# Scale and shift of three norms moved from a GpSimd run to a VectorE job that advances between weight splits

## The chip, the cores and the metric

The kernel runs on one core of one Trainium2 chip. A core has five engines that each take their own list of instructions in order and wait for one another by semaphores: TensorE (PE, matrix products), VectorE (DVE), ScalarE (ACT), GpSimd (POOL) and SyncE (SP, which here only issues transfers). The metric is the device time of one execution in microseconds (us), as the median of several runs.

## The reference

One layer of a streaming encoder on 256 frames of width 2048, all in float32. `P` below is a block of 128 rows; the residual stream `x` is normalised four times.

```
x = LN(x) * ln_in_g + ln_in_b
mix = concat(mLSTM heads, conv channels, chunked attention heads)(x @ w_in) @ w_out
x = LN(ALPHA * x + mix) * ln1_g + ln1_b
ca = softmax((x @ xq) @ k^T) @ v @ xo            # k, v = mem @ xkv
x = LN(ALPHA * x + ca) * ln2_g + ln2_b
gate, val = x @ ffn_w_up ; gate = causal_conv3(gate)
x = LN(ALPHA * x + (gelu(gate) * val) @ ffn_w_down) * ln3_g + ln3_b
```

## The kernel before

**Precision.** Every large product is made of three products of float32r parts: a matrix is split into `hi` (a rounded copy) and `lo` (the rest), and hi·hi, hi·lo and lo·hi are added up. The activations are split once. The weights stream through: `load_w` fetches a tile `raw` (three buffers, filled by transfers that SP issues), and cuts it into two halves; for each half ACT casts `hi` and DVE subtracts `lo` (function `split`, line 156), into four pairs of buffers (seven in the feed-forward part). So a half is ready for TensorE when its `lo` is, and a `raw` buffer is free for the next transfer when both of its halves have been split.

**The two forms of product.** `tm_part` (line 209) takes the weights as the moving operand and needs `lo` at its second matmul of a half. `cm_chunk` (lines 176 and 182) takes them as the stationary operand, with the eight hi matmuls of a half first and the eight lo matmuls behind; in the feed-forward part it holds all lo matmuls of a chunk back behind its four hi halves.

**Jobs.** Work that belongs beside the products (norms, attention heads, the convolution) is written as generators in the list `jobs`. Each product calls `tick` once per half, and `tick` advances every job by one step. Within an engine a scheduler then sets the final order, with a few instructions pinned by `keep_in_program_order`, all of POOL's transfers among them (`pool_load`).

**The stage in question.** The residual stream lies in `xt` as two tiles of 128 tokens by 2048 columns. What the products read next is a transposed copy that gets its scale and shift in ACT (`ln_transpose`), so TensorE never waits for the scale and shift of `xt` itself: `xt` needs it only by the next residual sum, hundreds of microseconds later. `ln_affine` does this for the input norm, the norm behind the mixer and the norm behind the cross attention, once the normalised stream is transposed. For each of four blocks of 512 columns (called rounds below) POOL loads the scale row and the shift row, copied to all partitions, into the single buffer `gb` (the two transfers are called the scale load and the shift load below), then multiplies and adds for both token tiles: 16 instructions of 128x512 for a norm on POOL, which has little else to do there.

The first norm's run lies under the first part of the input projection. There `tm_part` takes the weights in eight halves of 784 columns, eight of 768 and four of 1024, called the first to the twentieth half below; the second run lies under the key projection (`cm_chunk`), the third under the first chunks of the feed-forward part.

Of the kernel before, what the change touches and what calls it, by code (L numbers as in the profile page):

```python
# [52 lines left out]
def trunk_kernel(ctx: ExitStack, tc: tile.TileContext, plan, x, memT, wts, pvec, rows, gbias, abias, normg, out):  # L53
    nc = tc.nc
    V, A, G = nc.vector, nc.scalar, nc.gpsimd
# [81 lines left out]


    jobs = []

    def tick():
        for j in list(jobs):
            if next(j, jobs) is jobs:
                jobs.remove(j)

    def drain():
        while jobs:
            tick()
# [15 lines left out]
    def cm_chunk(a, mat, c0, c1, dst, loaded=None):  # L164

        ps = mm.tile([P, 2, 2, S], F32, name="mm")
        cols = [slice(j * P, (j + 1) * P) for j in range(2)]  # L170
        held = 4 if len(homes) > 4 else 1
        lows = []
        for ks, wH, wL in loaded or cm_load(mat, c0, c1):
            for kk, k in enumerate(ks):
                for j, cs in enumerate(cols):
                    nc.tensor.matmul(ps[:, j], lhsT=wH[:, kk, cs], rhs=a[:, k], start=(k == 0), stop=(k == KT - 1),  # L176
                                     skip_group_check=True)
            lows += [(k, wL[:, kk]) for kk, k in enumerate(ks)]
            if len(lows) == held * len(ks):
                for k, w in lows:  # L180
                    for j, cs in enumerate(cols):
                        nc.tensor.matmul(ps[:, j, 0, :], lhsT=w[:, cs], rhs=a[:, k, 0, :], start=False,  # L182
                                         stop=(k == KT - 1), skip_group_check=True)
                lows = []
            tick()
        cm_close(ps, dst)
# [11 lines left out]
    def tm_part(ps, a, mat, ks, cols, first=True, last=True, row0=0):  # L198

        n = sum(b - a for a, b in cols)  # L200
        kg = 8 if n <= 256 else 4
        for g in range(0, len(ks), kg):
            for kl, wH, wL in load_w(mat, [row0 + k for k in ks[g:g + kg]], cols):
                for kk, kr in enumerate(kl):
                    k = kr - row0
                    for tt in range(NT):
                        tsl = slice(tt * P, (tt + 1) * P)
                        for i, (part, w) in enumerate(((0, wH), (0, wL), (1, wH))):
                            nc.tensor.matmul(ps[tt][:, :n], lhsT=a[:, k, part, tsl], rhs=w[:, kk, :],  # L209
                                             start=(first and k == ks[0] and i == 0), stop=(last and k == ks[-1] and i == 2))  # L210
                tick()
# [95 lines left out]
    def ln_job(a, names, ri, wait):  # L307
        mv, rs = ln_scales(4)
        ln_normalise(mv, rs, 0)
        for _ in range(wait):  # L310
            yield
        for c in range(4):
            if c < 3:
                ln_normalise(mv, rs, c + 1)
            for k2 in range(4 * c, 4 * c + 4, 2):
                ln_transpose(a, names[0], names[1], k2)
            yield
        ln_affine(ri, rs)

    def pool_load(dst, src):  # L320

        tc.keep_in_program_order(G.dma_start(dst, src))
# [3 lines left out]
    def ln_affine(ri, begin):  # L326

        begun.append(tc.keep_in_program_order(G.tensor_copy(small.tile([P, NT], F32, name="begun"), begin)))
        for c in range(4):
            gb = lnp.tile([P, 2, 512], F32, name="gb")  # L330
            for i in range(2):
                pool_load(gb[:, i, :], rows[ri + i, c * 512:(c + 1) * 512].partition_broadcast(P))
            for tt in range(NT):
                sl = xt[:, tt, c * 512:(c + 1) * 512]
                G.tensor_mul(sl, sl, gb[:, 0, :])  # L335
                G.tensor_add(sl, sl, gb[:, 1, :])  # L336


    def load_mem(mp, g):
# [359 lines left out]


    def residual(ps, c, cols, first=True, last=True, tts=range(NT)):
        n = cols[c][1] - cols[c][0]
        for tt in tts:
            sl = xt[:, tt, cols[c][0]:cols[c][1]]
            if first:
                V.scalar_tensor_tensor(sl, sl, ALPHA, ps[tt][:, 0:n], ALU.mult, ALU.add)
            else:
                V.tensor_add(sl, sl, ps[tt][:, 0:n])
            if last:
                V.bn_stats(stats[:, tt, c, :], sl)  # L710

    mp = act_parts()
    for c in range(2):
        tm_part(ps01[c], mix, "w_out", list(range(4)), [COLS[c]], first=False)
        load_mem(mp, c)
        residual(ps01[c], c, COLS)
    for c in range(2, 4):
        ps = tm_open()
        tm_part(ps, mix, "w_out", list(range(KT)), [COLS[c]])
        load_mem(mp, c)  # L720
        residual(ps, c, COLS)
# [75 lines left out]
    for c in range(2):  # L797
        tm_part(ps01[c], op, "xo", list(range(12, 16)), [COLS_LAST[c]], first=False)
        residual(ps01[c], c, COLS)
# [3 lines left out]
    with tc.tile_pool(name="pre", bufs=1) as pre:  # L803
# [43 lines left out]
        behind.extend([[split0[3][0], split1[1]]] * 2 + [split1] * 2)  # L847
        up1 = list(cm_load("up", P, DFF + P))
    ln_affine(4, xp[:, KT - 1, 1, S - NT:S].bitcast(F32))


# [36 lines left out]
    for tt in range(NT):  # L888
        for c in (3, 4):
            n = COLS_LAST[c][1] - COLS_LAST[c][0]  # L890
            sl = xt[:, tt, COLS_LAST[c][0]:COLS_LAST[c][1]]
# [3 lines left out]
        for c in range(4):  # L895
            cs = slice(c * 512, (c + 1) * 512)
            sl = xt[:, tt, cs]
# [53 lines left out]
```

## Time and profile before

| | |
|---|---|
| median of three runs | 1525.84 us (1525.41 to 1526.14) |
| the profiled execution, its own time | 1525.82 us |
| its span, first to last instruction | 1523.6 us |
| TensorE busy | 1506.2 us, 99% of the span |
| VectorE busy | 1022.2 us, 67% |
| ScalarE busy | 764.3 us, 50% |
| GpSimd busy | 134.9 us, 9% |
| mean granted TensorE clock | 0.997 of full speed |

A busy share says how much of the span an engine had an instruction in it. TensorE's matmuls overlap, and one that waits inside a run of others shows as a gap between two starts. What a stall of another engine costs is therefore read from the starts of TensorE's rows, against the time at which each operand was ready.

### The profile page before, as it was taken

The numbers are of one execution on the slowest core, as the hardware profiler recorded it, in microseconds if no ns is written. First come the engines' busy times: TensorE is split into PE (matmuls) and PEld (weight loads), VectorE is DVE, ScalarE is ACT, GpSimd is POOL, SyncE is SP. The second block draws the span as 40 slices with busy tenths as digits, with TensorE's granted clock in tenths as the row PEclk, the third lists the DMA queues.
The fourth block names the chain that finished last, engine by engine and source line by source line (L and its number), as shares of the span: only waits on it lengthen the run. The fifth ranks groups of instructions, "written<-read, shape, count | busy, mean of one in ns | idle before, by whom it ended". The sixth has DMA issues, their size and how long they took to land.

```text
span 1523.6 us, 20632 instructions
## 1 busy us (share of the span) xinstructions
PE 1506.2 (99%) x8254; PEld 1314.2 (86%) x8254; DVE 1022.2 (67%) x1346; ACT 764.3 (50%) x1000; POOL 134.9 (9%) x133
## 2 busy tenths in 40 slices
PE   9999999999999999999999999999999999999996
PEld 7998888888888888998898888888888888888886
DVE  7875999688686545665678765566656665566666
ACT  6554454685454445554455643455435554455541
POOL 0460001000006300000027000000000000000000
PEclk9999999999999999999999999999999999999998
DMA  8585555454656654435647555545554545545451
GB/s 342 177 263 198 184 188 181 153 197 163 238 199 216 217 197 169 163 139 193 221 162 226 222 182 205 193 166 209 185 192 186 195 179 196 206 166 211 169 190 66
DMA packets 46351, 293.39 MB, mean 193 GB/s; under 512 B 5484, under 2 KB 6128, under 8 KB 15536
## 3 DMA queue, kind: packets, MB, share of 16 engines
q1 hardware_dynamic: 42768, 282.12, 50.6%
q0 software_dynamic: 2768, 8.66, 2.8%
q8 instruction: 64, 1.05, 0.3%
q10 hardware_dynamic: 720, 1.31, 0.2%
q14 instruction: 31, 0.25, 0.1%
HBM read 289.97 MB, written 2.10 MB: 192 GB/s over the span
## 4 chain that ended last, share of the span: by engine, by line
PE 93%; DVE 4%; DMA 2%; ACT 2%; issue 0%; SPq 0%; ACTq 0%; DVEq 0%
PE mm L209 37%; PE mm L176 33%; PE mm L182 17%; DVE lo L156 2%; DMA raw<-wts_in 2%; PE mm L236 1%; PE aux L751 1%; PE aux L781 1%; PE aux L288 0%; ACT y L302 0%; ACT hi L156 0%; DVE xt L899 0%; DVE xt L898 0%; DVE ac L871 0%; PE aux L570 0%
## 5 line engine op out<-in xcount | busy, mean ns | idle before, releaser
L156 DVE TENSOR_TENSOR lo<-raw,hi 128x1024 fp32r<-128x1024 f32 (+3 forms) x528 | 642.0, 1239 | 340.5 <-ACT hi L156 260.0
L156 ACT CAST hi<-raw 128x1024 fp32r<-128x1024 f32 (+3 forms) x528 | 540.6, 1027 | 493.3 <-PE mm L209 254.1
L176 PE MATMUL mm<-parts,hi 128*128 128x512 f32 x2400 | 582.0, 393 | 0.4 <-DVE gv L192 0.4
L176 PEld LDWEIGHTS mm<-parts,hi 128*128 128x128 f32 x2400 | 440.2, 188 | 86.8 <-DVE gv L192 0.6
L182 PEld LDWEIGHTS mm<-parts,lo 128*128 128x128 f32 x2400 | 308.0, 190 | 13.7 <-DVE lo L156 0.2
L209 PE MATMUL mm<-hi,parts 128*128 128x512 f32 (+3 forms) x1088 | 315.8, 372 | 0.0
L182 PE MATMUL mm<-parts,lo 128*128 128x256 f32 x2400 | 312.1, 281 | 0.0
L209 PEld LDWEIGHTS mm<-hi,parts 128*128 128x128 f32 x1088 | 200.1, 189 | 32.6 <-ACT hi L156 0.3
L209 PE MATMUL mm<-hi,hp 128*128 128x512 f32 x660 | 205.7, 392 | 0.0
L209 PE MATMUL mm<-lo,parts 128*128 128x512 f32 (+3 forms) x544 | 202.2, 372 | 0.8 <-DVE lo L156 0.8
L209 PEld LDWEIGHTS mm<-hi,hp 128*128 128x128 f32 x660 | 123.9, 188 | 26.7
L209 PE MATMUL mm<-lo,hp 128*128 128x512 f32 x330 | 128.4, 389 | 0.0
L209 PEld LDWEIGHTS mm<-lo,parts 128*128 128x128 f32 x544 | 102.7, 189 | 17.0 <-DVE lo L156 1.1
L189 ACT COPY gv<-mm 128x512 f32<-128x512 f32 x44 | 25.8, 587 | 100.0 <-PE mm L182 97.2
L871 DVE SCALAR_TENSOR_TENSOR ac<-gv,pv,ac 128x255 f32<-128x255 f32 x88 | 47.5, 540 | 41.1 <-ACT ac L868 39.6
L209 PEld LDWEIGHTS mm<-lo,hp 128*128 128x128 f32 x330 | 62.0, 188 | 13.6
L509 DVE SCALAR_TENSOR_TENSOR cac<-cpad,pv,cac 128x256 f32<-128x256 f32 x120 | 51.3, 480 | 0.0
L336 POOL TENSOR_TENSOR xt<-xt,gb 128x512 f32<-128x512 f32 x24 | 47.9, 2015 | 1.4 <-DMA gb<-rows_in 1.4
L335 POOL TENSOR_TENSOR xt<-xt,gb 128x512 f32<-128x512 f32 x24 | 42.5, 1791 | 43.2 <-DMA gb<-rows_in 36.2
L868 ACT ACTIVATE ac<-gv,pv 128x256 f32<-128x256 f32 x44 | 26.3, 598 | 26.5 <-DVE gv L192 26.5
L873 DVE TENSOR_TENSOR ac<-gv,ac 128x256 f32<-128x256 f32 x44 | 18.7, 425 | 28.3 <-ACT ac L872 28.3
L156 DVE TENSOR_TENSOR hp<-ac,hp 128x256 fp32r<-128x256 f32 x44 | 18.7, 426 | 21.6 <-ACT hp L156 21.6
(242 smaller groups left out, 772.4 us busy)
## 6 DMA issues: line engine op xcount, KB each, us to landing
raw<-wts_in SPq DMA_DIRECT2D x238, 1024.0 KB, 4.9
raw<-wts_in SPq DMA_DIRECT2D x19, 768.0 KB, 4.4
gb<-rows_in POOLq DMA_DIRECT2D x24, 256.0 KB, 5.0
raw<-wts_in SPq DMA_DIRECT2D x4, 784.0 KB, 4.6
raw<-wts_in SPq DMA_DIRECT2D x6, 512.0 KB, 7.8
xt<-x_in SPq DMA_DIRECT2D x4, 512.0 KB, 11.0
raw<-memT_in SPq DMA_DIRECT2D x4, 512.0 KB, 3.6
gb<-rows_in SPq DMA_DIRECT2D x2, 1024.0 KB, 5.4
```

What stands on the lines that cost most here:

```text
L156: for ins in (A.copy(hi, src), V.tensor_sub(lo, src, hi.bitcast(F32))):
L176: nc.tensor.matmul(ps[:, j], lhsT=wH[:, kk, cs], rhs=a[:, k], start=(k == 0), stop=(k == KT - 1), skip_group_check=True)
L182: nc.tensor.matmul(ps[:, j, 0, :], lhsT=w[:, cs], rhs=a[:, k, 0, :], start=False, stop=(k == KT - 1), skip_group_check=True)
L189: copy = A.copy(dst, ps[:, :, 1, :])
L209: nc.tensor.matmul(ps[tt][:, :n], lhsT=a[:, k, part, tsl], rhs=w[:, kk, :], start=(first and k == ks[0] and i == 0), stop=(last and k == k ...
L236: nc.tensor.matmul(ps[tt][c][:, :n], lhsT=a[:, k, part, tt * P:(tt + 1) * P], rhs=w[:, kk, :], start=(k == ks[0] and i == 0), stop=(k == k ...
L335: G.tensor_mul(sl, sl, gb[:, 0, :])
L336: G.tensor_add(sl, sl, gb[:, 1, :])
L509: tap = V.scalar_tensor_tensor(cac[:, i, :], cpad[:, i, j:j + S], pcol("ccw", i * CT + j), cac[:, i, :], ALU.mult, ALU.add)
L868: A.activation(ac, gv[:, 0, :], AF.Identity, bias=pcol("fcb", f), scale=pcol("fcw", f * 3 + 2))
L871: V.scalar_tensor_tensor(ac[:, o:], gv[:, 0, 0:S - o], pcol("fcw", f * 3 + t), ac[:, o:], ALU.mult, ALU.add)
L873: V.tensor_mul(ac, gv[:, 1, :], ac)
```

## The change

The rounds are no longer issued as one run on POOL. `ln_affine` puts a generator, `affine_job`, into a second list, `slow`, which `tick` advances behind `jobs` and which `drain` doesn't wait for. A round now has the two loads on POOL as before, four ticks of nothing, and then for each token tile one multiply and one add on DVE and a tick. `gb` still has one buffer, so the loads of the next round wait for the last add of this one.

```diff
     jobs = []
+    slow = []
 
     def tick():
-        for j in list(jobs):
-            if next(j, jobs) is jobs:
-                jobs.remove(j)
+        for some in (jobs, slow):
+            for j in list(some):
+                if next(j, some) is some:
+                    some.remove(j)
...
     def ln_affine(ri, begin):
 
         begun.append(tc.keep_in_program_order(G.tensor_copy(small.tile([P, NT], F32, name="begun"), begin)))
+        slow.append(affine_job(ri))
+
+    def affine_job(ri):
         for c in range(4):
             gb = lnp.tile([P, 2, 512], F32, name="gb")
             for i in range(2):
                 pool_load(gb[:, i, :], rows[ri + i, c * 512:(c + 1) * 512].partition_broadcast(P))
+            for _ in range(4):
+                yield
             for tt in range(NT):
                 sl = xt[:, tt, c * 512:(c + 1) * 512]
-                G.tensor_mul(sl, sl, gb[:, 0, :])
-                G.tensor_add(sl, sl, gb[:, 1, :])
+                V.tensor_mul(sl, sl, gb[:, 0, :])
+                V.tensor_add(sl, sl, gb[:, 1, :])
+                yield
...
     def residual(ps, c, cols, first=True, last=True, tts=range(NT)):
+        assert not slow
```

The order of instructions changes on DVE and POOL, and on ACT in one place (a cast in the feed-forward part); on TensorE and SP it is the same as before. The line numbers of the changed kernel are higher by two and later by eight or nine. Tiles carry the numbers of their own program.

On DVE under the input projection, before, from the fifth half (the first row) to the eleventh:

```order
L156 TENSOR_TENSOR lo_701<-raw_698,hi_700 128x784
L156 TENSOR_TENSOR lo_717<-raw_698,hi_716 128x784
L156 TENSOR_TENSOR lo_735<-raw_732,hi_734 128x784
L156 TENSOR_TENSOR lo_751<-raw_732,hi_750 128x784
L156 TENSOR_TENSOR lo_778<-raw_775,hi_777 128x768
L156 TENSOR_TENSOR lo_794<-raw_775,hi_793 128x768
L156 TENSOR_TENSOR lo_818<-raw_815,hi_817 128x768
```

The same place in the changed kernel, from the fifth half to the eleventh, with the multiplies (L342) and adds (L343) of the first two rounds:

```order
L158 TENSOR_TENSOR lo_678<-raw_675,hi_677 128x784
L158 TENSOR_TENSOR lo_696<-raw_675,hi_695 128x784
L342 TENSOR_TENSOR xt_90<-xt_90,gb_577 128x512 x2
L343 TENSOR_TENSOR xt_90<-xt_90,gb_577 128x512 x2
L158 TENSOR_TENSOR lo_717<-raw_714,hi_716 128x784
L158 TENSOR_TENSOR lo_733<-raw_714,hi_732 128x784
L158 TENSOR_TENSOR lo_760<-raw_757,hi_759 128x768
L342 TENSOR_TENSOR xt_90<-xt_90,gb_711 128x512 x2
L343 TENSOR_TENSOR xt_90<-xt_90,gb_711 128x512
L158 TENSOR_TENSOR lo_776<-raw_757,hi_775 128x768
L343 TENSOR_TENSOR xt_90<-xt_90,gb_711 128x512
L158 TENSOR_TENSOR lo_802<-raw_799,hi_801 128x768
```

The seventh half (now `lo_717`) stands behind all of round one, the tenth (now `lo_776`) behind three of the four instructions of round two. The later rounds stand likewise: the thirteenth half is behind the first multiply of round three, the fourteenth behind all of it and five small gate instructions, the sixteenth behind the first multiply of round four and the seventeenth behind its next two instructions.

On DVE under the key projection, in the changed kernel, from the second half of round two to the end of round four (before, only the `lo` and `kT` rows stood here, one behind another):

```order
L158 TENSOR_TENSOR lo_4341<-raw_4318,hi_4340 128x1024
L194 TENSOR_TENSOR kT_3899<-kT_3899,mm_4181 128x512
L343 TENSOR_TENSOR xt_90<-xt_90,gb_4315 128x512
L158 TENSOR_TENSOR lo_4366<-raw_4363,hi_4365 128x1024
L342 TENSOR_TENSOR xt_90<-xt_90,gb_4451 128x512
L158 TENSOR_TENSOR lo_4386<-raw_4363,hi_4385 128x1024
L343 TENSOR_TENSOR xt_90<-xt_90,gb_4451 128x512
L342 TENSOR_TENSOR xt_90<-xt_90,gb_4451 128x512
L158 TENSOR_TENSOR lo_4410<-raw_4407,hi_4409 128x1024
```

`lo_4386` and `lo_4410` now stand behind parts of round three; behind these come the last add of it, `lo_4432`, a `kT` sum, both multiplies of round four and then `lo_4460`.

On POOL under the input projection, in the changed kernel, the loads of all four rounds follow one another with no arithmetic between them:

```order
L330 COPY begun_575<-rs_411 128x2
L324 DMA gb_577<-rows_in 128x512 x2
L324 DMA gbt_597<-gbias_in 128x8
L324 DMA gb_711<-rows_in 128x512 x2
L324 DMA gb_837<-rows_in 128x512 x2
L324 DMA gb_984<-rows_in 128x512 x2
```

Each pair from the second on waits for DVE's last add of the round before, where it waited for POOL's own.

## Rows read from the trace of the kernel before

**Rows 1.** The page: busy us, share of the span and instructions of each engine.
```profile
PE 1506.2 (99%) x8254; PEld 1314.2 (86%) x8254; DVE 1022.2 (67%) x1346; ACT 764.3 (50%) x1000; POOL 134.9 (9%) x133
```

**Rows 2.** TensorE's waits for DVE: us in total, times, longest.
```profile
PE mm L209 <- DVE lo L156: 0.8, 1, 0.8
PE mm L176 <- DVE gv L192: 0.4, 1, 0.4
```

**Rows 3.** Timeline of TensorE, input projection: start, us, engine, line, operation, tiles.
```profile
55.88 0.34 PE L209 MATMUL mm<-lo,parts 128*128 128x392 f32 x1
...
68.68 0.34 PE L209 MATMUL mm<-lo,parts 128*128 128x392 f32 x1
```

**Rows 4.** Timeline of DVE, around the start of the first run.
```profile
48.76 0.69 DVE L293 TENSOR_TENSOR parts<-y,parts 128x512 fp32r<-128x512 f32 x1
49.37 0.42 DVE L292 CAST parts<-y 128x512 fp32r<-128x512 f32 x1
...
60.91 3.67 DVE L156 TENSOR_TENSOR lo<-raw,hi 128x784 fp32r<-128x784 f32 x3 [0.31 <-ACT hi L156]
65.31 0.98 DVE L156 TENSOR_TENSOR lo<-raw,hi 128x784 fp32r<-128x784 f32 x1 [0.74 <-ACT hi L156]
```

**Rows 5.** Chain that ended last, key projection: start, us, what.
```profile
486.64 0.95 PE mm L182 x8
...
489.44 0.95 PE mm L182 x8
...
495.02 0.95 PE mm L182 x8
```

**Rows 6.** Timelines of DVE and TensorE, start of the feed-forward part.
```profile
787.32 4.62 DVE L156 TENSOR_TENSOR lo<-raw,hi 128x1024 fp32r<-128x1024 f32 x4
...
803.17 6.82 DVE L156 TENSOR_TENSOR lo<-raw,hi 128x1024 fp32r<-128x1024 f32 x4
...
809.10 3.97 PE L182 MATMUL mm<-parts,lo 128*128 128x256 f32 x32
...
835.61 7.60 PE L176 MATMUL mm<-parts,hi 128*128 128x512 f32 x32 [0.41 <-DVE gv L192]
```

**Rows 7.** Timeline of POOL: loads of round one and two, and of the second norm.
```profile
62.79 1.26 POOL L322 DMA_DIRECT2D gb<-rows_in  x2
...
75.15 1.11 POOL L322 DMA_DIRECT2D gb<-rows_in  x2 [0.30 <-POOL xt L336]
...
462.63 1.09 POOL L322 DMA_DIRECT2D gb<-rows_in  x2
```

**Rows 8.** Pairs of gb loads, first norm then second, one row a round, issue to landing.
```profile
DMA to landing us min/median/max: 4.6/6.3/8.0
...
DMA to landing us min/median/max: 5.5/7.2/8.9
...
DMA to landing us min/median/max: 5.1/6.4/7.6
...
DMA to landing us min/median/max: 4.2/5.2/6.1
...
DMA to landing us min/median/max: 5.5/6.2/6.9
...
DMA to landing us min/median/max: 4.8/5.3/5.8
...
DMA to landing us min/median/max: 4.3/5.5/6.6
...
DMA to landing us min/median/max: 4.9/5.1/5.3
```

**Rows 9.** Third norm, its first three pairs of gb loads.
```profile
DMA to landing us min/median/max: 4.1/4.4/5.8
```

**Rows 10.** Windows: busy us of PE, PEld, DVE, ACT, POOL, then granted clock, DMA, GB/s.
```profile
10.00:14.00 4.00, 3.24 (x15) 2.25 (x14) 2.74 (x4) 2.94 (x4) 0.00 (x0) 1.00 1.03 412
...
1512.00:1523.00 11.00, 0.00 (x0) 0.00 (x0) 8.01 (x18) 0.29 (x1) 0.00 (x0) 0.55 0.32 119
```

## The prediction

> **What bounds the kernel now.** I read the page's busy times first. TensorE is busy for 1506.2 of 1523.6 us [rows 1], so what can be won is small, and whatever makes TensorE wait is lost in full: behind it there is no slack in which it could be made up. The second view is the list of waits. TensorE waits for DVE twice in the whole kernel, 0.8 us at the start, before any norm, and 0.4 us [rows 2]; the second is the 0.41 us at 835.6 in the feed-forward part, under the last POOL run [rows 6]. The third view is TensorE's timeline under the first run. The first `lo` matmul of the input projection starts at 55.88 us and that of the seventh half at 68.68 [rows 3], so a half of 784 columns takes 12.80 / 6 = 2.13 us and one of 768 about 2.13 x 768/784 = 2.09, with no gap although POOL works beside it. Under the second run the chain is an unbroken row of TensorE pieces too [rows 5]. So the POOL runs cost this kernel about 0.41 us now, and the question is whether DVE can take their work without being late with a `lo`.
>
> **The work itself.** 48 instructions of 128x512 leave POOL and come to DVE. A multiply or subtract of that size on DVE takes 0.69 us alone, and the next starts 0.61 us behind it [rows 4]: 48 x 0.61 = 29 us on an engine that is busy for 67% of the span. DVE gets something back. Four `lo` of 1024 columns took 4.62 us where POOL did no arithmetic and 6.82 us where it did [rows 6], 0.55 us more for each. The Trainium skill, "SBUF — State Buffer", section "Who interferes with whom", says that a DVE instruction with two SBUF inputs and a GpSimd instruction that reads SBUF shut each other out; the trace agrees in kind (6.82 against 4.62 us). By that rule the change would only help, since it ends all such meetings; its worth to TensorE would be the same 0.41 us. I take -0.4 us for it.
>
> **The wait that is added.** DVE works in order. In the changed order (shown above) the first multiply of a round waits on DVE for the scale load and the first add for the shift load, and the `lo` of the next halves stand behind them. Before, the same waits stood on POOL, which had nothing else to do. The loads stay on POOL. A round's loads can be issued only when DVE's last add of the round before is done; I allow 0.3 us for that, as between POOL's own last add and its next load [rows 7]. From issue to landing the first of a pair (scale) took 4.2 to 5.5 us and the second (shift), which is issued some 0.6 us later, 5.3 to 8.9 us under the first two norms [rows 8], and 4.1 to 5.8 under the third [rows 9]; in each row the least is the scale load's and the most the shift load's. So a round is at least some 5 us of waiting, and the `lo` that DVE may do meanwhile are those that the order puts there: two to three. A `lo` that is done early helps no more than its four buffers reach.
>
> **First norm.** The first loads are issued at 62.79 and about 63.4 [rows 7]; nothing ahead of them changes. For the loads I take 4.6 and 6.0 us, about the middle of the rows: the largest, 8.0 and 8.9, were landed beside weight transfers that will now be held back, because a `raw` buffer comes free only when DVE has split it. A `lo` of 784 columns takes 0.96 us (0.98 in the row) [rows 4].
> Round one: scale lands at 67.4, two multiplies until 68.6, shift lands at 69.4, two adds until 70.6, the seventh half's `lo` at 71.6. TensorE wants it at 68.7: it waits 2.9 us. Before, that `lo` was among the three done by 64.58 [rows 4].
> Round two: issued at 70.9, scale at 75.5. DVE does three halves until 73.5 and stands still until then; two multiplies, the shift at 77.5, one add until 78.1, the tenth half at 79.1. TensorE, 2.9 us late, wants it at 78.0: 1.1 us.
> Round three: last add of round two 79.7, loads 80.0, scale 84.6, multiply, a small gate instruction, the thirteenth half at 86.4, wanted at 85.4: 1.0. Then an add, a multiply and an add with the shift at 86.6, with small gate instructions between, and the fourteenth half at 89.7, wanted at 88.4: 1.3.
> Round four: issued at 88.9, scale 93.5, multiply, the sixteenth half at 95.1, wanted at 93.9: 1.2. Add and multiply, the seventeenth half at 97.9, wanted at 97.1: 0.7.
> Sum 8.2 us. With every load as in its own row it is 14.9 (round one alone 4.9, round two 4.0); with all loads as fast as under the third norm (4.2, and 4.5 to 5.8) 5.5.
>
> **Second norm.** Here a half is 2.79 us and `lo` is wanted only behind its eight hi matmuls, so DVE may be some 8 us behind. With the loads' own rows, from the issue at 462.63 [rows 7]: scale 468.1, shift 470.1, last add, behind one `lo`, 472.0; round two loads 472.3, scale 477.1, shift 478.7, last add 481.7, with no half late yet; round three loads 482.0, scale 486.3, one multiply, `lo_4386` at 488.0. TensorE wants it at 486.64 [rows 5]: 1.4 us. Shift 489.1, add, multiply, `lo_4410` at 491.5, wanted at 489.44 + 1.4: 0.7. Last add 492.1, round four's scale 497.3, two multiplies, `lo_4460` at 499.7, wanted at 495.02 + 2.1: 2.6. Sum 4.7 us; with loads as under the third norm 0.7, with 4.6 and 6.0 it is 3.1.
>
> **Third norm.** The four `lo` of the first chunk are split before round one, and the second chunk's are wanted from 809.1 on [rows 6], when by the loads of [rows 9] round two is over at about 802.5 and DVE has done them at 806. DVE reaches the `gv` sum that held TensorE at 835.6 some microseconds earlier than before. No wait, and the 0.4 us are won.
>
> **Sum.** 8.2 + 4.7 - 0.4 = +12.5 us on the profiled execution's own 1525.82 (span 1523.6 and 2.2 around it), which is the median of the runs shown to 0.02 us: 1538.3 us. Taking the arithmetic from POOL is worth nothing by itself.
>
> **Rivals.**
> *The queue's waits are covered, result 1527.5 or less.* This decides if the loads land so early that only round one is late: 2.1 us with a scale at 67.4 and a shift right behind it, less 0.4. For it speaks that later rounds miss by only 0.7 to 1.4 us each; against it that each round's start hangs on the one before, so a miss is carried on, and that no scale load took under 4.1 us.
> *Not slower: the shared access is what counted, result 1525.4.* DVE gets back 0.55 us for each `lo` beside POOL, and TensorE no longer waits at 835.6. It wins only if all waits together stay under 0.4 + 3.05 us. Against it stands round one: 62.79 + 4.6 + four instructions + a `lo` is 70.8 even with a shift load that costs nothing, over 2 us late. Faster by 3 us can hardly come from here, since TensorE's waits for DVE are 1.2 us in all.
> *Much slower, about 1550.* The second norm's loads are as slow as the first's (9.2 us instead of 4.7) beside 14.9 in the first: 14.9 + 9.2 - 0.4 = +23.7, 1549.5. The granted clock could add to it. It was 1.00 across an idle 0.76 us of TensorE, and 0.55 in the last 11 us, where TensorE does nothing [rows 10]; a half at 1.2 GHz would cost 2.1 us more. The Trainium skill, "TensorE: Matmul & The Clock Gate", Part 1, has the clock fall when the array idles and come back with work; no row here has an idle time of 1 to 5 us in the middle of products, so what it does there is open, and I put no price of it into the sum.
>
> **Numbers.** Slower by the queue's waits 0.82, much slower 0.06, only round one 0.06, not slower 0.06. A difference under 0.2% (3.05 us) is about what a measurement of this kernel can't tell from none. Slower 0.88, same 0.08, faster 0.04. The range goes from the fast loads (5.5 + 0.7 - 0.4 = +5.8, 1531.6) to the slow ones (14.9 + 4.7 - 0.4 = +19.2, 1545.0), a little wider at both ends for the cases beyond: 1530 to 1546.
>
> **What would show it.** Right: TensorE's waits list names DVE `lo` at line 209 and 176 or 182 with some 13 us, six of them between 68 and 100 us and two or three near 490 to 505; DVE's waits list names the `gb` transfers under lines 342 and 343; four `lo` under the third norm take 4.6 us again; the wait for `gv` is gone. Wrong, if round one's adds end before 68 us, if TensorE waits at the feed-forward start, or if the granted clock falls behind one of the waits.

## The result and the profile after

| | before | changed |
|---|---|---|
| median of 4 runs each | 1525.62 us (1524.82 to 1526.14) | 1544.37 us (1543.80 to 1544.93) |
| profiled execution, its own time | 1525.82 us | 1543.80 us |
| its span | 1523.6 us | 1541.8 us |
| TensorE busy / idle in the span | 1506.2 / 17.4 us | 1512.8 / 29.0 us |

The changed kernel is slower by 18.75 us, a ratio of 1.0123 (95% interval 1.0111 to 1.0135). The forecast was 1538.3, with a range up to 1546.

The page of the changed kernel, its busy line (answers to [rows 1]) and its chain, shares of the span:

```profile
PE 1512.8 (98%) x8254; PEld 1318.1 (85%) x8254; DVE 1024.0 (66%) x1394; ACT 763.0 (49%) x1000; POOL 44.6 (3%) x85
...
PE 90%; DMA 4%; DVE 3%; ACT 1%; POOL 1%; issue 1%; SPq 0%; DVEq 0%; ACTq 0%; POOLq 0%
PE mm L211 34%; PE mm L178 33%; PE mm L184 17%; DMA gb<-rows_in 3%; PE mm L238 1%; DMA raw<-wts_in 1%; DVE lo L158 1%; PE aux L760 1%; PE aux L790 1%; PE mm L848 1%; POOL parts L295 1%; PE mm L851 0%; DVE xt L908 0%; DVE xt L907 0%; DVE xt L343 0%
```

POOL gave up 90 us of work and VectorE is busy for only 1.8 us more, since its `lo` beside POOL run shorter. What is new is in the chain: the `gb` loads, which only POOL waited for, hold 3% of the time that sets the end.

The list of waits of the changed kernel, TensorE's for DVE (answers to [rows 2]):

```profile
PE mm L211 <- DVE lo L158: 10.2, 7, 4.8
PE mm L184 <- DVE lo L158: 2.4, 1, 2.4
```

And DVE's for the loads:

```profile
DVE xt L342 <- DMA gb<-rows_in: 28.5, 10, 4.9
...
DVE xt L343 <- DMA gb<-rows_in: 7.7, 6, 2.9
```

DVE stands still for 36.2 us for loads, and 11.4 us of that reaches TensorE (12.6 against 1.2 before). This is not all: TensorE is also busy 6.6 us longer with the same 8254 instructions. Idle +11.6 and busy +6.6 make the +18.2 of the span.

DVE's timeline of the changed kernel around round one (answers to [rows 4]), and round four's first add:

```profile
60.68 2.79 DVE L158 TENSOR_TENSOR lo<-raw,hi 128x784 fp32r<-128x784 f32 x2 [0.31 <-ACT hi L158]
66.95 1.29 DVE L342 TENSOR_TENSOR xt<-xt,gb 128x512 f32<-128x512 f32 x2 [3.49 <-DMA gb<-rows_in]
71.17 1.29 DVE L343 TENSOR_TENSOR xt<-xt,gb 128x512 f32<-128x512 f32 x2 [2.92 <-DMA gb<-rows_in]
72.38 2.72 DVE L158 TENSOR_TENSOR lo<-raw,hi 128x784 fp32r<-128x784 f32 x3
...
99.68 0.69 DVE L343 TENSOR_TENSOR xt<-xt,gb 128x512 f32<-128x512 f32 x1 [2.05 <-DMA gb<-rows_in]
```

The chain that ended last, pieces in order of time, of the same stretch: start, us, what.

```profile
63.27 7.80 DMA gb<-rows_in
...
73.29 5.55 DMA gb<-rows_in
...
81.39 6.33 DMA gb<-rows_in
...
92.19 7.40 DMA gb<-rows_in
```

From 60 us until TensorE's matmul at 102.16 the chain does not touch TensorE at all. It goes from a load to DVE's multiply or add, through it to the next round's load, and so on. A load that is in the chain from its issue takes 5.55 to 7.80 us.

TensorE's timeline of the changed kernel (answers to [rows 3]): the waiting `lo` matmul of the seventh, thirteenth, fourteenth, sixteenth and seventeenth halves and what follows the first, then `lo_4386` under the second norm.

```profile
73.40 0.69 PE L211 MATMUL mm<-lo,parts 128*128 128x392 f32 x1 [4.79 <-DVE lo L158]
73.89 0.85 PE L211 MATMUL mm<-hi,parts 128*128 128x392 f32 x2
...
78.39 0.34 PE L211 MATMUL mm<-lo,parts 128*128 128x392 f32 x1
78.57 0.51 PE L211 MATMUL mm<-hi,parts 128*128 128x392 f32 x2
...
89.43 0.44 PE L211 MATMUL mm<-lo,parts 128*128 128x384 f32 x1 [0.96 <-DVE lo L158]
...
92.36 0.44 PE L211 MATMUL mm<-lo,parts 128*128 128x384 f32 x1 [0.58 <-DVE lo L158]
...
97.68 0.45 PE L211 MATMUL mm<-lo,parts 128*128 128x384 f32 x1 [0.89 <-DVE lo L158]
...
102.16 0.58 PE L211 MATMUL mm<-lo,parts 128*128 128x256 f32 x1 [2.18 <-DVE lo L158]
...
503.62 1.22 PE L184 MATMUL mm<-parts,lo 128*128 128x256 f32 x8 [2.43 <-DVE lo L158]
504.68 3.38 PE L178 MATMUL mm<-parts,hi 128*128 128x512 f32 x8
```

Look at the row behind the first wait: a pair of matmuls takes 0.85 us at 73.89 and 0.51 at 78.57. The windows of the changed kernel show why; the columns are those of [rows 10], and the granted clock stands ahead of the DMA share.

```profile
65.00:70.00 5.00, 3.61 (x21) 3.29 (x19) 1.29 (x2) 1.72 (x3) 0.00 (x0) 1.00 0.70 234
70.00:75.00 5.00, 1.60 (x5) 1.60 (x6) 3.83 (x5) 0.00 (x0) 1.07 (x2) 0.65 0.16 32
75.00:80.00 5.00, 5.00 (x22) 5.00 (x21) 2.47 (x5) 0.83 (x2) 0.00 (x0) 0.67 0.87 229
80.00:85.00 5.00, 5.00 (x30) 5.00 (x29) 3.85 (x7) 3.29 (x5) 1.07 (x2) 1.00 0.64 209
```

Behind the wait the granted clock is between its two levels on the mean of five microseconds, so a part of these matmuls ran at 1.2 GHz. From 73.40 to 78.39 fifteen matmuls take 4.99 us; at the pace of [rows 3], 2.13 us for a half of 12, they take 2.7. That is 2.3 us on top of a wait of 4.79.

### The profile page after: what moved, and what is told of

Read it like the earlier page. It is cut to its first block, busy times and chain, and to the rows that moved or that the text cites. A ratio compares the mean times of both kernels' runs of the same rounds, so it can differ in the third digit from the quotient of the medians.

```text
span 1541.8 us, 20624 instructions
## 1 busy us (share of the span) xinstructions
PE 1512.8 (98%) x8254; PEld 1318.1 (85%) x8254; DVE 1024.0 (66%) x1394; ACT 763.0 (49%) x1000; POOL 44.6 (3%) x85
## 4 chain that ended last, share of the span: by engine, by line
PE 90%; DMA 4%; DVE 3%; ACT 1%; POOL 1%; issue 1%; SPq 0%; DVEq 0%; ACTq 0%; POOLq 0%
PE mm L211 34%; PE mm L178 33%; PE mm L184 17%; DMA gb<-rows_in 3%; PE mm L238 1%; DMA raw<-wts_in 1%; DVE lo L158 1%; PE aux L760 1%; PE aux L790 1%; PE mm L848 1%; POOL parts L295 1%; PE mm L851 0%; DVE xt L908 0%; DVE xt L907 0%; DVE xt L343 0%
## 5 line engine op out<-in xcount | busy, mean ns | idle before, releaser
L158 DVE TENSOR_TENSOR lo<-raw,hi 128x1024 fp32r<-128x1024 f32 (+3 forms) x528 | 622.3, 1202 | 323.1 <-ACT hi L158 243.3
L880 DVE SCALAR_TENSOR_TENSOR ac<-gv,pv,ac 128x255 f32<-128x255 f32 x88 | 42.5, 483 | 40.9 <-ACT ac L877 39.4
L342 DVE TENSOR_TENSOR xt<-xt,gb 128x512 f32<-128x512 f32 x24 | 15.9, 688 | 28.5 <-DMA gb<-rows_in 28.5
L158 ACT CAST hp<-ac 128x256 fp32r<-128x256 f32 x44 | 17.9, 406 | 24.9 <-DVE ac L882 24.9
```

The costliest lines, as they stand in the source:

```text
L158: for ins in (A.copy(hi, src), V.tensor_sub(lo, src, hi.bitcast(F32))):
L342: V.tensor_mul(sl, sl, gb[:, 0, :])
L880: V.scalar_tensor_tensor(ac[:, o:], gv[:, 0, 0:S - o], pcol("fcw", f * 3 + t), ac[:, o:], ALU.mult, ALU.add)
```

## The experiments

Three theories stood against one another. **Place**: DVE comes to a round before its loads have landed, and the `lo` queued behind pay for it. **Work**: 29 us of arithmetic on DVE make the `lo` late, wherever it stands. **Clock**: part of the time is no wait at all, but slower products behind waits. The first four kernels ran on one chip, against 27 runs of the kernel before (1526.39 us, 1525.39 to 1528.31).

### The same work, later and pinned

Nothing leaves DVE; multiplies and adds are held at their place in the program, and a round comes later behind its loads.

```diff
-            for _ in range(4):
+            for _ in range(6 if c else 9):
                 yield
...
-                V.tensor_mul(sl, sl, gb[:, 0, :])
-                V.tensor_add(sl, sl, gb[:, 1, :])
+                tc.keep_in_program_order(V.tensor_mul(sl, sl, gb[:, 0, :]))
+                tc.keep_in_program_order(V.tensor_add(sl, sl, gb[:, 1, :]))
```

> All 48 multiplies and adds stay on DVE and gb keeps one buffer, but each is pinned behind what DVE has been given before it in the program, and a round waits nine ticks (the first) or six after its loads, so the loads land before DVE comes to the arithmetic. If DVE's standing still for the gb loads is the cause, TensorE has no new wait and the kernel takes 1525.2 to 1527 us, with the 0.4 us wait for gv gone. If DVE's 29 us of added arithmetic makes the lo late, it stays above 1538 us.

Measured: 1525.13 us (1524.61 to 1525.78, 11 runs), 0.07 us under the expected range, ratio 0.9991 (0.9982 to 1.0000), span 1522.8. First the busy line, then TensorE's waits for DVE, then DVE around round one, of this kernel:

```profile
PE 1505.3 (99%) x8254; PEld 1313.7 (86%) x8254; DVE 1025.2 (67%) x1394; ACT 763.8 (50%) x1000; POOL 44.4 (3%) x85
```

```profile
PE mm L211 <- DVE lo L158: 1.0, 2, 0.8
```

```profile
60.65 3.66 DVE L158 TENSOR_TENSOR lo<-raw,hi 128x784 fp32r<-128x784 f32 x3 [0.31 <-ACT hi L158]
...
68.05 0.69 DVE L342 TENSOR_TENSOR xt<-xt,gb 128x512 f32<-128x512 f32 x1
69.72 0.69 DVE L343 TENSOR_TENSOR xt<-xt,gb 128x512 f32<-128x512 f32 x1 [0.98 <-DMA gb<-rows_in]
```

All 48 instructions are still on DVE, and the whole loss is gone. The seventh half's `lo` is again one of three that end by 64.3, ahead of round one. This refutes the work theory. Two things changed at once here, the ticks and the pinning; the pinned kernel with four ticks, below, takes them apart. It is also the fastest version by its ratio, but not one that can be told from the kernel before.

### Nearly no work, same loads and order of the code

The multiplies and adds touch 2 of 512 columns; scale and shift of the other 510 are left out.

```diff
-                sl = xt[:, tt, c * 512:(c + 1) * 512]
-                V.tensor_mul(sl, sl, gb[:, 0, :])
-                V.tensor_add(sl, sl, gb[:, 1, :])
+                sl = xt[:, tt, c * 512:c * 512 + 2]
+                V.tensor_mul(sl, sl, gb[:, 0, 0:2])
+                V.tensor_add(sl, sl, gb[:, 1, 0:2])
```

> The changed kernel, but each multiply and add works on 2 of the 512 columns, so scale and shift are left out for the others. The 48 waits on the gb loads stay on DVE, and their arithmetic shrinks from 29 us to about 6 us. If the waits are the cause, the time stays near the changed kernel's, 1536 to 1546 us (each round is some 2 us shorter, but the shorter work is also put closer together). If the arithmetic is the cause, it falls to 1525 to 1530 us.

Measured: 1550.28 us (1549.20 to 1551.18, 4 runs), ratio 1.0152 (1.0137 to 1.0168), span 1549.2. Taking the work out made the kernel slower still, which none of the theories had in its numbers. DVE's waits for the loads, and its rounds under the second norm, of this kernel:

```profile
DVE xt L342 <- DMA gb<-rows_in: 42.2, 12, 6.4
```

```profile
481.75 0.23 DVE L342 TENSOR_TENSOR xt<-xt,gb 128x2 f32<-128x2 f32 x2 [5.37 <-DMA gb<-rows_in]
...
488.29 0.23 DVE L342 TENSOR_TENSOR xt<-xt,gb 128x2 f32<-128x2 f32 x2 [3.88 <-DMA gb<-rows_in]
...
495.44 0.23 DVE L342 TENSOR_TENSOR xt<-xt,gb 128x2 f32<-128x2 f32 x2 [3.36 <-DMA gb<-rows_in]
...
502.98 0.23 DVE L342 TENSOR_TENSOR xt<-xt,gb 128x2 f32<-128x2 f32 x2 [4.30 <-DMA gb<-rows_in]
```

A round still lasts 6.5 to 7.5 us, since the loads set its length, but DVE does only one or two `lo` in it, which is 2.8 to 5.6 us of TensorE's time at 2.79 a half. In the changed kernel the rounds stood 8.5 to 10.9 us apart with two or three `lo` in each. DVE's waits for the scale load grew from 28.5 to 42.2 us, and now TensorE waits under the third norm too (4.0 us of its 8.9 for line 184). That shorter instructions let the scheduler put the rounds closer together is how I read the two orders; that arithmetic is not the price is shown. Of the span's 25.6 us more, 19.0 are idle time of TensorE, and 6.6 are longer busy time (1512.8 us), as much as in the changed kernel.

### The pieces, back on POOL

The job stays, in pieces between half tiles, but its multiplies and adds run on POOL (`V.` becomes `G.` in the two lines).

> The changed kernel with its job in pieces, ticks and loads as they are, but the multiplies and adds on POOL. If only DVE's wait in its queue matters, the time is that of the kernel before, 1525 to 1526.5 us. If the cutting into pieces, the second list or the later program places were to blame, it stays several us above 1526.

Measured: 1525.82 us (1524.67 to 1529.93, 10 runs), ratio 0.9998 (0.9989 to 1.0007). TensorE waits for a `lo` only the 0.8 us at the start. So the generator, the later places and the loads by themselves cost nothing that the runs can show; the loss needs DVE to be the engine that waits.

### One norm alone

The job serves one norm; the other two keep the POOL run, `affine_run`. For the third norm:

```diff
-        slow.append(affine_job(ri))
+        if ri == 4:
+            slow.append(affine_job(ri))
+        else:
+            affine_run(ri)
```

> Only the norm before the feed-forward part goes to DVE; the first two stay runs on POOL as before. By the queue theory nothing is late there and the 0.4 us wait for gv is gone: 1525.0 to 1525.6 us, and four lo of 1024 columns take 4.6 us throughout. If each norm's move costs about the same, a third of the 18.7 us is left: 1531 to 1533 us.

Measured: 1525.60 us (1524.88 to 1526.25, 11 runs), ratio 0.9993 (0.9984 to 1.0002). The wait for `gv` of [rows 6] is gone, and no other has come under the third norm. (Two small ones, 0.22 us at 8.52 and 0.38 at 86.06, lie far ahead of it, where the job is not at work.) A gain of 0.4 us is below what the runs can show.

The next three kernels ran on another chip, against 9 runs of the kernel before (1525.90 us, 1525.29 to 1528.04). The same edit with `ri == 0`, the first norm:

> Only the input norm's scale and shift go to DVE, as in the changed kernel; the other two stay runs on POOL. By the queue theory its waits (9.4 us) and the two stretches of lowered clock under it make 14 us, as the traces shift there: 1538 to 1541 us. If each norm costs a third: 1532.

Measured: 1537.85 us (1536.45 to 1540.02, 4 runs), ratio 1.0077 (1.0063 to 1.0091), +11.95 us. The first norm carries the most. The time is just under the expected 1538 to 1541, and one of the two slow stretches did not come. Waits for `lo` are 9.3 us in the list, 0.8 of it at the start as before, TensorE is busy 3.0 us longer (1509.2), and together 8.5 + 3.0 are 11.5 of the span's +11.9. Two of its waits on TensorE's timeline, and the windows behind them:

```profile
72.77 0.45 PE L211 MATMUL mm<-lo,parts 128*128 128x392 f32 x1 [3.17 <-DVE lo L158]
...
101.48 0.38 PE L211 MATMUL mm<-lo,parts 128*128 128x256 f32 x1 [2.09 <-DVE lo L158]
```

```profile
75.00:80.00 5.00, 5.00 (x24) 5.00 (x23) 2.87 (x5) 1.83 (x3) 0.00 (x0) 0.76 0.66 215
...
100.00:105.00 5.00, 3.52 (x29) 3.52 (x30) 5.00 (x7) 3.07 (x5) 0.00 (x0) 1.00 0.34 128
```

The clock fell behind the first and not behind the second, although a wait of about the same length there (2.18 us, window 0.72) slowed the changed kernel. So this term comes and goes from wait to wait.

### Pinned, but as early as in the change

Four ticks as in the change; only the order is held, by the same two lines as in the first experiment.

> The changed kernel with its four ticks, but each multiply and add pinned behind what DVE has been given before it in the program. Round one under the first norm stands where it stood (behind the sixth half); the later rounds come behind five halves instead of two or three, later than their loads land. By the queue theory one wait is left, that for the seventh half, 4.8 us as in the changed kernel, and its lowered clock (fifteen matmuls took 2.3 us more there): 1525.6 - 0.4 + 7.1 = 1532.3, in 1530 to 1534 us. If the arithmetic or the mere presence of the pieces cost time, it is above 1538.

Measured: 1531.50 us (1530.39 to 1532.49, 5 runs), ratio 1.0035 (1.0021 to 1.0048), span 1528.6. Round one stands at the same place as in the change; the later rounds, no longer pulled ahead, hold up no `lo` that TensorE wants in this profile. One wait of 3.26 us is left, and behind it ten matmuls take 3.41 us instead of 1.78: 3.26 + 1.6 = 4.9 of the span's +5.0.

```profile
72.63 0.70 PE L211 MATMUL mm<-lo,parts 128*128 128x392 f32 x1 [3.26 <-DVE lo L158]
```

The expected wait was 4.8 us with 2.3 of slow products; the time still fell into the range. So with the pinning alone 5.6 of the 18.75 us are left, and the longer distance of the first experiment removes these. This made a clean place to measure the clock term.

### The same wait, with TensorE kept at work

Products that nobody reads (the 128x128 identity with itself) are put on TensorE ahead of the seventh half's matmuls, 42 of them:

```diff
+    def fill(n):
+        ps = aux.tile([P, 512], F32, name="aux")
+        for _ in range(n):
+            last = tc.keep_in_program_order(nc.tensor.matmul(ps[:, 0:P], lhsT=ident, rhs=ident, start=True, stop=True))
+        return tc.issue_after(last.ins)
...
+                with filled(mat, {("w_in", 6): 42}):
                     for kk, kr in enumerate(kl):
```

> The kernel with the four ticks pinned, and 42 matmuls of 128x128 on the identity (some 4.6 us of TensorE, results unused) before the seventh half, where TensorE would stand idle for 4.8 us. DVE, ACT and POOL have the same order. If the idle time itself lowers the granted clock, the matmuls behind the wait run at full speed and the kernel is 1.5 to 2.5 us faster than without them. If the slow matmuls have another cause (the data arriving late, the transfers), it is the same or, by what the added matmuls overrun, up to 1 us slower.

Measured: 1534.51 us (1534.33 to 1535.35, 5 runs), ratio 1.0055 (1.0043 to 1.0068). The filling was too long. The row of it in this kernel's timeline of TensorE:

```profile
68.56 9.54 PE L94 MATMUL aux<-ident 128*128 128x128 f32 x84
```

Each of the 42 ran as two matmuls, and together they outlast the wait they were to fill by several microseconds. Behind them pairs take 0.51 us, but the kernel is 3.0 us slower than the unfilled one, which neither branch had, and the times settle nothing. So I cut it to 16 and ran it beside its unfilled twin on a third chip (before: 1525.93 us, 11 runs).

> As the filled kernel before, with 16 in place of 42 added matmuls: each of them ran as two of 0.11 us there, so 42 were 9.3 us and overran the wait by some 5 us; 16 are 3.5 us, just under the time until the seventh half's lo is ready. If idle time lowers the granted clock, the matmuls behind the wait run at full speed and the kernel is 1.6 us faster than the one without added matmuls (ten matmuls took 3.4 instead of 1.8 us there), near 1530 us. If not, it is the same.

> The kernel with the four ticks pinned once more, as the partner of the filled one on the same chip: 1531.5 us as before, 1.6 us slower than the filled one if the clock falls by idle time, the same if not.

Measured: filled 1530.21 us (1528.33 to 1531.30, 7 runs), ratio 1.0028 (1.0017 to 1.0039); unfilled 1531.47 us (1531.00 to 1532.47, 5 runs), ratio 1.0038 (1.0024 to 1.0052). TensorE's timeline of the unfilled kernel at the seventh half:

```profile
73.61 0.69 PE L211 MATMUL mm<-lo,parts 128*128 128x392 f32 x1 [4.79 <-DVE lo L158]
74.10 0.85 PE L211 MATMUL mm<-hi,parts 128*128 128x392 f32 x2
...
76.97 0.52 PE L211 MATMUL mm<-hi,parts 128*128 128x392 f32 x2
...
79.46 0.34 PE L211 MATMUL mm<-lo,parts 128*128 128x384 f32 x1
```

And of the filled one:

```profile
68.51 3.74 PE L94 MATMUL aux<-ident 128*128 128x128 f32 x32
...
73.75 0.45 PE L224 MATMUL mm<-lo,parts 128*128 128x392 f32 x1 [1.32 <-DVE lo L170]
74.04 0.51 PE L224 MATMUL mm<-hi,parts 128*128 128x392 f32 x2
...
75.64 0.53 PE L224 MATMUL mm<-hi,parts 128*128 128x392 f32 x2
...
78.14 0.34 PE L224 MATMUL mm<-lo,parts 128*128 128x384 f32 x1
```

The windows from 75 us on, of the unfilled kernel and then of the filled one, with the granted clock ahead of the DMA share:

```profile
75.00:80.00 5.00, 5.00 (x25) 5.00 (x24) 2.95 (x5) 1.35 (x3) 0.00 (x0) 0.81 0.76 222
```

```profile
75.00:80.00 5.00, 5.00 (x30) 5.00 (x29) 3.78 (x6) 2.01 (x4) 0.00 (x0) 1.00 0.77 213
```

The `lo` comes 0.14 us later in the filled kernel (73.75 against 73.61), and yet the ninth half starts 1.32 us earlier (78.14 against 79.46). The ten matmuls behind the wait take 1.89 us instead of 3.36, and the granted clock stays at 1.00 where it was 0.81. TensorE had the same operands at nearly the same time; what it did during the wait is the difference between the two programs, and this is worth 1.5 us, with 1.4 us in the spans and 1.26 us between the medians, whose ranges overlap. So the clock term is real and apart from the wait: 1.5 us here, on top of 4.79.

## Why the prediction came out as it did

Direction and cause were right: DVE waits for loads that nobody waited for before, and the half weight tiles behind it pay. The sum was 6 us short: the first norm's waits and above all the clock were more than forecast, the second norm's waits less.

**The first norm's waits, 8.2 forecast, 9.4 measured.** By halves, forecast against measured: seventh 2.9 and 4.79, tenth 1.1 and none, thirteenth 1.0 and 0.96, fourteenth 1.3 and 0.58, sixteenth 1.2 and 0.89, seventeenth 0.7 and 2.18. The step that failed is "the largest, 8.0 and 8.9, were landed beside weight transfers that will now be held back". The scale load of round one landed as I took it (DVE's multiply at 66.95, taken 67.4), but the shift load of round one took 7.80 us and that of round four 7.40, where I took 6.0 for both. The windows show where the reason failed in round one: a weight tile of 768 KB was issued at 63.5 us, beside the shift load, and took 7.8 us to land; all transfers together moved 234 GB/s from 65 to 70 us, and only from 70 us, when both were nearly down, did they fall to 32. The own-row bound of round one, 4.9 us, was the better figure. The load itself varies: the pinned program with four ticks saw 6.28 us and a wait of 3.26 in one profile, 7.82 us and 4.79 in the other, with 238 GB/s from 65 to 70 us in both, so what makes it vary stays open. The thirteenth's term came out by luck: round three's scale load took 6.33 us, not 4.6, and its issue came 1.4 us later than forecast, but TensorE was 3.1 us later too. The tenth half did not wait since TensorE, 4.79 us late and then slow, wanted it later than I had it; the same lateness shortened the fourteenth's.

**The second norm's waits, 4.7 forecast, 2.4 measured, and the time lost there, 4.6.** `lo_4386` waited 2.43 us instead of 1.4: round three's scale load took 4.9 us and not 4.3, and its issue came 0.5 us later than forecast (both counted from the norm's first load), since round two's shift load took 6.37 us and not 5.8. Behind it `lo`, hi and `lo` take 5.42 us (503.62 to 509.04) where the full pace gives 0.95 + 1.84 + 0.95 = 3.74 [rows 5]. Those 1.7 us of slow products and the first wait made TensorE late enough that `lo_4410` and `lo_4460`, forecast at 0.7 and 2.6, were ready in time; for `lo_4460` a scale load of 4.1 us instead of 4.9 helped. The 4.6 us lost in this stage are near the forecast 4.7 by luck: part of what I had as waits came as clock.

**The clock, priced at nothing.** "What it does there is open, and I put no price of it into the sum" was the step that cost most: TensorE is busy 6.6 us longer, and three stretches show 5.6 us of it directly: 2.3 behind the seventh half, 1.6 behind the seventeenth (fifteen matmuls from 102.16 in 3.37 us, at full pace 1.8) and 1.7 behind `lo_4386`. The prediction named a fall of the granted clock behind a wait as a sign that it was wrong, and that sign came. Of the waits named as signs of being right, five came instead of six under the first norm, and one instead of two or three under the second. The Trainium skill, "TensorE: Matmul & The Clock Gate", Part 1, "HAM oscillation", describes products that wait for data between bursts and start each burst slow; the rows here agree in kind, and not for every wait.

**The third norm, -0.4 forecast, about -0.6 measured.** No wait came, and `gv`'s went. Right, and the third norm alone shows it as nothing measurable.

**DVE gets time back**, as said: four `lo` under the third norm take 4.62 us again, and DVE's busy time rises by 1.8 us instead of 29. The Trainium skill's rule ("SBUF — State Buffer", section "Who interferes with whom") held here (4.62 us again, against 6.82), and it was worth nothing that the end time shows, because DVE's arithmetic was not what TensorE waited for: the pinned late kernel, which has this gain too, ends where the kernel before does. DVE's row under the third norm, of the changed kernel:

```profile
806.20 4.62 DVE L158 TENSOR_TENSOR lo<-raw,hi 128x1024 fp32r<-128x1024 f32 x4
```

**The rivals.** "Not slower" had the price of the work right and the waits wrong. "Much slower, about 1550" was nearer in its clock than in its waits: the second norm's 9.2 us did not come.

Two counts close the account. The shifts are +14.2 us at the end of the first norm's stage (TensorE's first row of the next stage at 115.75, before at 101.53), +4.6 through the second, -0.6 through the third: +18.2, the span's. And 11.6 us of idle time plus 6.6 of longer busy time are the same 18.2. In the first stage 9.4 of waits and 3.9 of slow products make 13.3 of the 14.2; most of the rest lies in how a wait is counted, from the modelled end of the matmul before. By starts the seventh half's is 4.96 us: the pair ahead of it starts at 68.09, so the next was due at 68.44 and came at 73.40. What stays open is why the clock falls behind one wait and not behind another of the same length.

## What to carry to other kernels

Before work moves from an engine that nobody waits for to one that works in order and feeds the bounding engine, price what the work waits for, not how long it runs: here 48 instructions cost nothing that the runs can show, and the waits for their 24 loads, with the slow products behind the waits, cost 18.75 us. Place such work where its operands have landed, hold it there, and read the order that results, since a scheduler may move it up to the transfer it waits for. And count a stall of TensorE with the slow products that may follow it, a third (1.5 us on 4.79) to three quarters (1.6 on 2.18) of the stall again where they came here, and nothing in other places.

## What was not expected of the hardware

The granted clock did not follow the length of the wait. Behind waits of 4.79 us in two programs (the changed and the pinned one), 3.26, 3.17, 2.43 and 2.18 us matmuls ran slower for a while; in the two-column kernel a wait of 3.27 us, longer than four of these, was followed by pairs at 0.51 to 0.52 us and windows at 1.00, and one of 2.49 us under its second norm by a window at 1.00, while waits of 2.50 and 2.27 us under its first norm were followed by windows at 0.66. Nor does the fall keep to one place: in the changed kernel the first pair behind the 4.79 us is slow already (0.85 us), and with the first norm alone two pairs behind the 3.17 us still take 0.52 us before one takes 0.85, at 74.22. Behind those of 0.58 to 0.96 us no window was below 1.00. The rows that show the 3.27 us wait of that kernel:

```profile
72.32 0.45 PE L211 MATMUL mm<-lo,parts 128*128 128x392 f32 x1 [3.27 <-DVE lo L158]
72.61 0.52 PE L211 MATMUL mm<-hi,parts 128*128 128x392 f32 x2
```

A load of 256 KB copied to all partitions on POOL's queue took anything from 4.4 to 7.8 us under the first norm, and the same load in the same program 6.28 and 7.82 us in two profiles. And each added matmul, both of whose operands are plain float32, showed as two in the trace (32 rows for 16, 84 for 42), so filling by count came out at twice the length.
